# Spreading the norms' scales with two one-pass products, and loading the pooling weights in mid-kernel

## The chip, the core and the metric

The kernel runs on one core of one Trainium2 chip. The metric is the device time of one execution in microseconds, from the runs of the same kernel on that core; the median of three runs is quoted. Beside them stands one profiled execution, whose trace is read below. Its times are counted from the start of its span.

## The reference

One inference step of a two-layer trunk on 1024 prompt positions and 8 x 8 sample positions, width 1024, all in fp32. Cut to what matters here:

```python
def rms_norm(x, g):
    y = x * lax.rsqrt(jnp.mean(x * x, axis=-1, keepdims=True) + RMS_EPS)
    return y * g

# per layer l, x is (positions, 1024):
h = rms_norm(x, ng[MIX_PRE]);  y = mixer(h)          # even layer: pooling + convolution; odd: gated convolution
x = x + rms_norm(y, ng[MIX_POST])
h = rms_norm(x, ng[X_PRE]);    y = mem_attend(h)
x = x + rms_norm(y, ng[X_POST])
h = rms_norm(x, ng[FFN_PRE]);  y = conv_ffn(h)
x = x + rms_norm(y, ng[FFN_POST])

# the pooling head group of the even mixer ends in one 128 x 128 product per group g:
ya = einsum('bsgc,gcd->bsgd', pooled, w_pool) * pool_scale
```

So each position (a column in the kernel) has one scale per norm, and every norm multiplies 1024 channels by it.

## The kernel before, in words

Activations lie with the channels on the 128 partitions and the positions along the free axis. The positions are cut in two halves: half 0 has 512 prompt positions, half 1 has 512 prompt positions and the 64 samples (576, worked in two banks of 288). Three threads (`a` and `b` for the halves, `k` for the memory's keys and values) are Python generators. `schedule` (L461) runs them in an order written by hand (`SCRIPT`, L1457). Between pieces of matmul work, the norms, attention and convolutions run as background generators. When a background step is emitted depends on a planner, `Times` (L76): it keeps an estimated clock for each engine, and `after` (L319) lets a generator wait until TensorE's planned clock has come up to the planned end of a tile. `proj` (L499) calls the background after chunks 1, 3 and 5 of a product (`MID`, L1642). The planner prices a product at L171 by the type of its stationary operand, `max(n * 1.667 + 5, 222)` ns for fp32 and `max(n * 0.451 + 2.5, 107)` for fp32r. Those are constants of the program and decide order alone.

Weight products are done with fp32 numbers cut into two fp32r parts (a rounded high part, and the rest), in three one-pass products (`mm3`, L488). Each weight tile is loaded by SyncE into the ring `w` (10 buffers) as `wraw`, copied to `whi` by ScalarE, and subtracted to `wlo` by VectorE.

A norm goes through `rstd_gen` (L536). The sum of squares `acc` is summed over partitions by products with a column of ones (`psum_s`, L550), which puts the sums of 128 positions on 128 partitions and leaves 4 or 5 columns. `rsqrt` (L575) makes `r` out of them in eleven small VectorE instructions. The products at L557 then spread `r` back: the stationary operand is one column of `r` broadcast to 128 x 128, the moving one is the identity `ident`, and the result holds each position's scale on all partitions. It goes to the bank `psum_n`, or to `psum_r` and from there by ScalarE to the tile `rs`. These are native fp32 products, and each shows in the trace as two instructions. `prenorm_gen` (L608), `postnorm_gen` (L649), `ln_gen` (L871), `last_gen` (L1397) and `kv_thread` (L1001) use it, for 28 norms in all. The tiles of the norms are called `h` both where the scaled value is made and where it is cut in two.

The pooling weights (256 KB) are loaded into a constant tile `wp` by GpSimd's queue in `run` (L1435, L1436). In `even_in`, half 0 cuts them into `wpool` (L762, L763) with `split` (L529) after the background work has ended, and the four pooling products (L770) follow at once. The other temporary tiles come from `tt` (L360), a ring of 11 buffers.

In `run`, `cst` (all constants, the identity among them) is loaded by ScalarE's queue. VectorE then fills `ones` and `zero`, and ScalarE runs a first small activation on `zero` (L1430). Each engine takes its instructions in the order in which the program emits them.

Of the kernel before, what the change touches and what calls it, by code (L numbers as in the profile page):

```python
# [4 lines left out]
F32 = mybir.dt.float32  # L5
F32R = mybir.dt.float32r
I32 = mybir.dt.int32
AF = mybir.ActivationFunctionType
ALU = mybir.AluOpType
AX = mybir.AxisListType  # L10

P = 128
# [63 lines left out]
class Times:  # L76
# [58 lines left out]
    def run(self, engine, ns, outs, ins, port=False):  # L135
        t = self.start(engine, outs, ins)
        if engine == "sync":
            self.free["sync"] = t + 60
            self.free["dma"] = max(self.free["dma"], t) + ns
            t, engine = max(self.free["dma"], t + ns) + 2000, "dma"  # L140
        else:
            if port:
                t = self.port(engine, t, ns)
            t += ns
            self.free[engine] = t
        for a in ins:
            self.last[a.tensor.name] = max(self.last.get(a.tensor.name, 0.0), t)
        for a in outs:
            self.note(a, t, engine)
# [142 lines left out]
class Trunk:  # L292
# [243 lines left out]
    def rstd_gen(self, acc, n, out, dim, eps):  # L536


        nc = self.nc
        offs = []  # L540
        o = 0
        while o < n:
            offs.append((o, min(P, n - o)))
            o += P
        nt = len(offs)
        yield from self.after(acc)
        ps = self.bank(name="psum_s")
        for j, (o, m) in enumerate(offs):
            o = o + m - P
            nc.tensor.matmul(ps[:, j:j + 1], lhsT=acc[:, o:o + P], rhs=self.ones[:, 0:1])  # L550
        r = self.rsqrt(ps[:, :nt], nt, dim, eps)
        yield from self.after(r)
        for o, m in self.spans(n):
            pb = self.bank(name="psum_r") if out is not None else self.norm_bank()
            for i in range(o // P, -(-(o + m) // P)):
                w = min(P, o + m - i * P)
                nc.tensor.matmul(pb[:, i * P - o:i * P - o + w], lhsT=r[:, i:i + 1].to_broadcast([P, P]),  # L557
                                 rhs=self.ident[:, P - w:], start=True, stop=True)
            if out is not None:
                nc.scalar.activation(out=out[:, o:o + m], in_=pb[:, :m], func=AF.Copy)  # L560
        yield
        return (pb if out is None else out)[:, :n]
# [145 lines left out]
    def even_in(self, th, H, ops, cat):  # L708
        nc = self.nc
        us = [None] * 4  # L710
        cbs = [self.s([P, 2, H.n], F32, "cb") for _ in range(2)]
        ready = [0] * 4
        L = CW - 1
        th.bg.append(self.conv_gen(H, us, cbs, ready))
        self.rank[th.bg[-1]] = CONV_RANK + H.i
        th.bg.append(self.ln_gen(H, cbs, ready, cat))
        for c in (0, 3, 2, 1):
            yield ("slots", 1)
            w = self.take(("in_even", 4 + c))
            b1 = self.proj(w, ops, H)  # L720
            yield "pe"
            w = self.take(("in_even", 8 + c))
            b2 = self.proj(w, ops, H)
            sg = self.tt(name="sg")
            for b, (o, n) in zip(b2, H.banks):
                nc.scalar.activation(out=sg[:, o:o + n], in_=b[:, :n], func=AF.Sigmoid)
            u = self.s([P, L + NP + NB * (L + 8) if H.i else L + NP], F32, "u")
            us_ = None
            if H.i == 0:
                nc.gpsimd.memset(u[:, 0:L], 0.0)  # L730
            else:
                nc.gpsimd.tensor_copy(out=u[:, 0:L], in_=self.carry_u[:, c, :])
                us_ = u[:, L + NP:].rearrange("p (b t) -> p b t", t=L + 8)
                nc.sync.dma_start(us_[:, :, 0:L], self.t["st_conf"][:, c])
            for bi, bo, n, to, kind in H.pieces:
                dst, like = u[:, L + to:L + to + n], lambda a: a
                if kind == "s":
                    dst, like = us_[:, :, L:], lambda a: a.rearrange("p (b t) -> p b t", t=8)
                nc.vector.tensor_tensor(out=dst, in0=like(b1[bi][:, bo:bo + n]), in1=like(sg[:, to:to + n]),
                                        op=ALU.mult)  # L740
            b1 = b2 = None
            if H.i == 0:
                nc.gpsimd.tensor_copy(out=self.carry_u[:, c, :], in_=u[:, NP:NP + L])
            else:
                nc.gpsimd.dma_start(self.t["o_conf_p"][:, c], u[:, NP:NP + L])
                nc.gpsimd.dma_start(self.t["o_conf_s"][:, c], us_[:, :, 8:])
            us[c] = (u, u[:, :L + NP], us_)
            del u
            yield "phase"
        pls = []  # L750
        for g in range(4):
            yield ("slots", 1)
            w = self.take(("in_even", g))
            b1 = self.proj(w, ops, H)
            pls.append(self.s([P, 2, H.n], F32R, "pl"))
            self.pool_chunk(th, H, g, b1, pls)
            yield "pe"
        ops.clear()
        yield "phase"
        yield "bg"  # L760
        if H.i == 0:
            self.wpool = self.s([P, 2, 4, P], F32R, "wpool")  # L762
            self.split(self.wpool.t, self.wp)  # L763
        for g in range(4):
            yield ("slots", 1)
            sc = self.const("pool_scale", g)
            x, c = pls[g], cat[g]
            for o, n in H.banks:
                b = self.bank()
                self.mm3(b[:, :n], (self.wpool[:, 0, g, :], self.wpool[:, 1, g, :]),  # L770
                         (x[:, 0, o:o + n], x[:, 1, o:o + n]), True, True)
                nc.scalar.activation(out=c[:, 0, o:o + n], in_=b[:, :n], func=AF.Copy, scale=sc)
                nc.vector.scalar_tensor_tensor(out=c[:, 1, o:o + n], in0=b[:, :n], scalar=sc,
                                               in1=c[:, 0, o:o + n].bitcast(F32), op0=ALU.mult, op1=ALU.subtract)
            pls[g] = x = None
        if H.i:
            self.wpool = None
        yield "pe"
# [640 lines left out]
    def run(self):  # L1419
        nc, t = self.nc, self.t  # L1420
        C = self.C
        self.cst = C.tile([P, N_CONST], F32, name="cst")
        nc.scalar.dma_start(self.cst, t["consts"])
        self.ident = self.const("ident", 0, P)
        self.ones = C.tile([P, P], F32, name="ones")
        nc.vector.memset(self.ones, 1.0)
        self.zero = C.tile([P, 1], F32, name="zero")
        nc.vector.memset(self.zero, 0.0)
        first = C.tile([P, 1], F32, name="first")
        nc.scalar.activation(out=first, in_=self.zero, func=AF.Square)  # L1430
        self.carry_u = C.tile([P, 4, CW - 1], F32, name="carry_u")
        self.carry_a = C.tile([P, 4, PB], F32, name="carry_a")
        self.carry_g = C.tile([P, 8, 2], F32, name="carry_g")
        self.carry_f = C.tile([P, NF, 2], F32, name="carry_f")
        self.wp = C.tile([P, 4, P], F32, name="wp")  # L1435
        nc.gpsimd.dma_start(self.wp, t["wpool"])  # L1436
        a, b, k = Thread("a"), Thread("b"), Thread("k")
        self.threads = [k, a, b]
        a.gen = self.half_thread(a, self.halves[0])
        b.gen = self.half_thread(b, self.halves[1])  # L1440
        k.gen = self.kv_thread(k)
        by_name = {"a": a, "b": b, "k": k}
        todo = {n: phases(n) for n in by_name}
        script = []
        for word in SCRIPT.split():
            n, _, times = word.partition("*")
            for _ in range(int(times or 1)):
                self.order += todo[n].pop(0)
                script.append(by_name[n])
        assert not any(todo.values()), todo  # L1450
        self.schedule(script)
        while any(th.bg for th in self.threads):
            self.background()
            self.idle(100)
# [26 lines left out]
def phases(thread):  # L1481

    if thread == "k":
        return [[]] + [[("%s%d" % (n, l), c + i) for i in range(2)] for l in range(2) for n in "kv" for c in range(0, 8, 2)]
    return [[]] + layer_units(0) + layer_units(1)
# [326 lines left out]
```

## Time and profile before

| what | value |
|---|---|
| median of 3 runs | 3032.44 us (3029.54 to 3032.87) |
| the profiled execution's own time | 3032.25 us |
| its span | 3030.5 us |
| mean granted TensorE clock | 0.992 |
| TensorE busy | 2962.4 us (98%), 17866 instructions |
| VectorE busy | 1936.1 us (64%) |
| ScalarE busy | 1286.3 us (42%) |
| GpSimd busy | 103.2 us (3%) |

PE is TensorE's matmul, PEld its weight load, DVE VectorE, ACT ScalarE, POOL GpSimd, SP SyncE; SPq and ACTq are the queues that issue their transfers. Nearly every instruction is recorded by one helper (L202), so the tiles' names tell the groups apart. A product's instructions overlap their neighbours: a burst of x instructions costs the time from its start to the start of what follows it, which is less than x times its mean.

### The profile page before, as it was taken

What the parts mean: (1) busy time and instruction counts of PE and PEld (TensorE: products, weight loads), DVE (VectorE), ACT (ScalarE), POOL (GpSimd) and SP (SyncE); (2) the same over time, 40 slices, a digit from 0 to 9 for tenths busy, and PEclk for the clock granted to TensorE, in tenths of its full rate; (3) what the DMA queues carried; (4) which work ended last, traced back from release to release, by engine and by line L of the source; (5) the groups of instructions that cost most, each with busy time, mean ns of one, the idle gap of its engine ahead of it and who ended that gap; (6) DMA issues with size and microseconds to landing.
All of it is one profiled execution on the core that took longest, in us unless ns stands there. A gap on an engine that the chain in (4) does not pass through costs nothing. (4 is left out here: it accounts for less than half of the span.)

```text
span 3030.5 us, 44401 instructions
## 1 busy us (share of the span) xinstructions
PE 2962.4 (98%) x17866; PEld 2686.9 (89%) x17866; DVE 1936.1 (64%) x3275; ACT 1286.3 (42%) x2027; POOL 103.2 (3%) x404
## 2 busy tenths in 40 slices
PE   7999999999999999999999999999999999999997
PEld 5998789888888999999988899989888989999997
DVE  7999955747737545557748374567477475555558
ACT  5333374555543432333334333545555444333332
POOL 1110000000000000000000000000000000000000
PEclk9999999999999999999999999999999999999998
DMA  6657535524543222223333332243355233222233
GB/s 239 205 155 254 192 115 207 206 94 161 177 167 128 86 84 91 91 79 111 111 114 133 98 133 89 81 167 115 115 174 169 89 128 103 81 83 84 91 99 134
DMA packets 126493, 396.27 MB, mean 131 GB/s; under 512 B 21152, under 2 KB 31840, under 8 KB 126288
## 3 DMA queue, kind: packets, MB, share of 16 engines
q1 hardware_dynamic: 120144, 372.67, 36.8%
q0 software_dynamic: 6000, 20.45, 1.8%
q8 instruction: 140, 2.29, 0.3%
q14 instruction: 65, 0.53, 0.1%
q10 hardware_dynamic: 144, 0.33, 0.0%
HBM read 338.08 MB, written 55.31 MB: 130 GB/s over the span
## 5 line engine op out<-in xcount | busy, mean ns | idle before, releaser
L202 PE MATMUL b<-h,whi 128*128 128x288 f32 (+1 forms) x6720 | 1618.2, 332 | 22.3 <-DVE h L202 17.1
L202 PEld LDWEIGHTS b<-h,whi 128*128 128x128 f32 x6720 | 1142.0, 190 | 120.6 <-DVE h L202 21.4
L202 PE MATMUL b<-h,wlo 128*128 128x288 f32 (+1 forms) x3360 | 1110.5, 331 | 0.8 <-DVE wlo L202 0.8
L202 DVE TENSOR_TENSOR wlo<-wraw,whi 128x1024 fp32r<-128x1024 f32 x396 | 484.8, 1224 | 337.7 <-ACT whi L202 333.2
L202 PEld LDWEIGHTS b<-h,wlo 128*128 128x128 f32 x3360 | 637.7, 190 | 52.2 <-DVE wlo L202 1.5
L202 ACT ACTIVATE whi<-wraw 128x1024 fp32r<-128x1024 f32 x432 | 451.2, 1049 | 246.9 <-PE b L202 227.8
L202 PE MATMUL b<-z,whi 128*128 128x288 f32 (+1 forms) x2112 | 503.4, 329 | 1.3 <-ACT z L202 0.9
L202 PEld LDWEIGHTS b<-z,whi 128*128 128x128 f32 x2112 | 357.3, 188 | 32.9 <-ACT z L202 1.2
L202 PE MATMUL b<-z,wlo 128*128 128x288 f32 (+1 forms) x1056 | 347.5, 329 | 0.0
L202 DVE SCALAR_TENSOR_TENSOR cv<-ext,cst,cv 128x512 f32<-128x512 f32 (+1 forms) x208 | 166.7, 801 | 275.9 <-ACT cv L202 272.0
L202 DVE TENSOR_TENSOR y<-y,b 128x288 f32<-128x288 f32 (+1 forms) x480 | 243.1, 530 | 86.7 <-PE b L202 84.5
L202 PEld LDWEIGHTS b<-z,wlo 128*128 128x128 f32 x1056 | 198.6, 188 | 15.9
L202 DVE SCALAR_TENSOR_TENSOR cb<-u,cst,cb 128x512 f32<-128x512 f32 x360 | 187.3, 597 | 0.4
L202 PE MATMUL b<-o,whi 128*128 128x288 f32 (+1 forms) x768 | 185.1, 332 | 1.3 <-ACT o L202 0.9
L202 PE MATMUL b<-cat,whi 128*128 128x288 f32 (+1 forms) x768 | 183.7, 330 | 0.2 <-DVE cat L202 0.2
L202 ACT ACTIVATE ext<-b 128x224 f32<-128x224 f32 (+3 forms) x176 | 65.2, 397 | 262.8 <-PE b L202 262.8
L202 DVE TENSOR_TENSOR acc<-acc,sq 128x576 f32<-128x576 f32 (+3 forms) x188 | 129.2, 690 | 57.4 <-ACT sq L202 54.8
L202 ACT ACTIVATE y<-b 128x288 f32<-128x288 f32 (+1 forms) x144 | 67.0, 472 | 216.4 <-PE b L202 216.4
L202 PEld LDWEIGHTS b<-o,whi 128*128 128x128 f32 x768 | 131.1, 190 | 12.7 <-ACT o L202 1.1
L202 PEld LDWEIGHTS b<-cat,whi 128*128 128x128 f32 x768 | 130.5, 189 | 12.4 <-DVE cat L202 0.6
L202 ACT ACTIVATE z<-z 128x512 fp32r<-128x512 f32 (+1 forms) x88 | 58.0, 659 | 194.9 <-DVE z L202 194.9
L202 PE MATMUL b<-o,wlo 128*128 128x288 f32 (+1 forms) x384 | 127.1, 331 | 0.0
(162 smaller groups left out, 2655.3 us busy)
## 6 DMA issues: line engine op xcount, KB each, us to landing
wraw<-w SPq DMA_DIRECT2D x464, 512.0 KB, 3.5
cache<-cache_k SPq DMA_DIRECT2D x32, 512.0 KB, 4.4
cache<-cache_v SPq DMA_DIRECT2D x32, 512.0 KB, 4.5
xd<-x SPq DMA_DIRECT2D x20, 576.0 KB, 6.9
x<-xd SPq DMA_DIRECT2D x20, 576.0 KB, 6.6
xd<-x SPq DMA_DIRECT2D x20, 512.0 KB, 6.0
x<-xd SPq DMA_DIRECT2D x20, 512.0 KB, 6.9
lo_in_even<-wlo POOLq DMA_DIRECT2D x12, 512.0 KB, 5.8
```

The costliest lines, as they stand in the source:

```text
L202: r = f(*args, **kw)
```

## The change

`rstd_gen` now copies `r` to an fp32r tile `rh` and the rest, `r - rh`, to `rl` on VectorE, and waits for `rl`. Each spreading product becomes two one-pass fp32r products, of `rh` and of `rl`, added in the bank. The moving operand is `unit`, an fp32r copy of the identity made on VectorE in `run`, ahead of `ones` and `zero`. The constant tile `wp` and its load on GpSimd's queue go. `even_in` takes a tile of the ring instead and loads the pooling weights on SyncE's queue just ahead of the split that reads them.

```diff
         r = self.rsqrt(ps[:, :nt], nt, dim, eps)
-        yield from self.after(r)
+        rh, rl = (self.R.tile([P, 8], F32R, tag=t, name=t)[:, :nt] for t in ("rh", "rl"))
+        nc.vector.tensor_copy(out=rh, in_=r)
+        nc.vector.tensor_tensor(out=rl, in0=r, in1=rh.bitcast(F32), op=ALU.subtract)
+        yield from self.after(rl)
         for o, m in self.spans(n):
             pb = self.bank(name="psum_r") if out is not None else self.norm_bank()
             for i in range(o // P, -(-(o + m) // P)):
                 w = min(P, o + m - i * P)
-                nc.tensor.matmul(pb[:, i * P - o:i * P - o + w], lhsT=r[:, i:i + 1].to_broadcast([P, P]),
-                                 rhs=self.ident[:, P - w:], start=True, stop=True)
+                for q in (rh, rl):
+                    nc.tensor.matmul(pb[:, i * P - o:i * P - o + w], lhsT=q[:, i:i + 1].to_broadcast([P, P]),
+                                     rhs=self.unit[:, P - w:], start=q is rh, stop=q is rl)
...
         if H.i == 0:
+            wp = self.tt(name="wp")[:, :4 * P].rearrange("p (g d) -> p g d", g=4)
+            self.nc.sync.dma_start(wp, self.t["wpool"])
             self.wpool = self.s([P, 2, 4, P], F32R, "wpool")
-            self.split(self.wpool.t, self.wp)
+            self.split(self.wpool.t, wp)
...
         self.ident = self.const("ident", 0, P)
+        self.unit = C.tile([P, P], F32R, name="unit")
+        nc.vector.tensor_copy(out=self.unit, in_=self.ident)
         self.ones = C.tile([P, P], F32, name="ones")
...
-        self.wp = C.tile([P, 4, P], F32, name="wp")
-        nc.gpsimd.dma_start(self.wp, t["wpool"])
```

## Rows read from the trace of the kernel before

**Rows 1.** The page, part 1: busy us by engine (share of the span), instructions.
```profile
PE 2962.4 (98%) x17866; PEld 2686.9 (89%) x17866; DVE 1936.1 (64%) x3275; ACT 1286.3 (42%) x2027; POOL 103.2 (3%) x404
```

**Rows 2.** Waits of the whole span: us in total, times, longest us.
```profile
PE b L202 <- DVE h L202: 17.1, 11, 2.5
```

**Rows 3.** Window: length; busy us (instructions) PE, PEld, DVE, ACT, POOL; granted clock, DMA share, GB/s.
```profile
2040.00:2044.00 4.00, 4.00 (x22) 4.00 (x23) 3.72 (x15) 0.35 (x1) 0.00 (x0) 0.63 0.00 0
```

**Rows 4.** Groups by form: instructions, shapes, count | busy us, mean ns | idle before.
```profile
L202 PEld LDWEIGHTS b<-h,whi 128*128 128x128 f32 x6720 | 1142.0, 190 | 120.6 <-DVE h L202 21.4 <-ACT whi L202 4.1 <-ACT h L202 1.4
...
L202 PEld LDWEIGHTS psum_r<-cst,r 128*128 128x128 f32 x130 | 16.4, 190 | 1.7 <-DVE r L202 0.8
...
L202 PEld LDWEIGHTS psum_n<-cst,r 128*128 128x128 f32 x110 | 15.9, 218 | 4.6 <-DVE r L202 4.5
```

**Rows 5.** Timeline around one norm, 310 to 316: start us, us, engine, operation.
```profile
310.81 0.95 PE L202 MATMUL psum_s<-ones,acc 128*128 128x1 f32 x8
...
311.62 3.70 PE L202 MATMUL b<-mop,wraw 128*128 128x256 f32 x16
...
313.58 0.16 DVE L202 SCALAR_TENSOR_TENSOR r<-q,r 128x4 f32<-128x4 f32 x1
...
315.16 1.05 PE L202 MATMUL psum_n<-cst,r 128*128 128x128 f32 x8
...
316.05 7.07 PE L202 MATMUL b<-mop,wraw 128*128 128x256 f32 x32
```

**Rows 6.** Timeline of PE around twelve fp32r products of 256 columns, 2089.8 to 2091.4.
```profile
2089.86 1.60 PE L202 MATMUL b<-kv,qx 128*128 128x256 f32 x12
...
2091.29 0.40 PE L202 MATMUL b<-h,whi 128*128 128x512 f32 x1
```

**Rows 7.** Timeline of the start, 0 to 15.
```profile
0.74 0.40 ACTq L202 DMA_DIRECT2D cst<-consts  x1
...
1.18 1.28 ACT L202 ACT_TABLE_LOAD   x1 [1.18 <-PEq L1800]
...
6.00 0.63 ACT L202 ACTIVATE acc<-x 128x512 f32<-128x512 f32 x1 [3.32 <-DMA x<-x]
...
7.18 0.69 DVE L202 TENSOR_TENSOR acc<-acc,sq 128x512 f32<-128x512 f32 x1 [6.17 <-ACT sq L202]
...
8.61 4.67 DVE L202 TENSOR_TENSOR acc<-acc,sq 128x512 f32<-128x512 f32 x6 [0.73 <-ACT sq L202]
...
13.33 1.86 PE L202 MATMUL psum_s<-ones,acc 128*128 128x1 f32 x8 [13.33 <-DVE acc L202]
```

**Rows 8.** Transfers: issues, KB each, median us from issue to landing.
```profile
kvraw<-kd SPq DMA_DIRECT2D x16, 256.0 KB, 4.2
...
cst<-consts ACTq DMA_DIRECT2D x1, 320.0 KB, 5.4
...
wp<-wpool POOLq DMA_DIRECT2D x1, 256.0 KB, 7.1
```

**Rows 9.** Timelines of four engines around the pooling products, 249 to 265.
```profile
249.57 2.45 SPq L202 DMA_DIRECT2D wraw<-w  x2
...
264.67 23.82 SPq L202 DMA_DIRECT2D wraw<-w  x7
...
252.92 0.62 ACT L202 ACTIVATE wpool<-wp 128x512 fp32r<-128x512 f32 x1
...
255.91 0.70 DVE L202 TENSOR_TENSOR wpool<-wp,wpool 128x512 fp32r<-128x512 f32 x1
...
256.67 2.60 PE L202 MATMUL b<-pl,wpool 128*128 128x512 f32 x10 [1.10 <-DVE wpool L202]
```

**Rows 10.** Timeline of DVE in the tail.
```profile
3015.64 0.16 DVE L202 TENSOR_TENSOR q<-q,y 128x3 f32<-128x3 f32 x1
...
3015.83 0.16 DVE L202 SCALAR_TENSOR_TENSOR r<-q,r 128x3 f32<-128x3 f32 x1
...
3026.32 0.82 DVE L202 TENSOR_TENSOR x<-x,h 128x288 f32<-128x288 f32 x2
```

## Prediction

> **What bounds the kernel.** I read the page first: TensorE is busy for 2962.4 us of 3030.5 (98%), VectorE for 64% [rows 1]. So a part of the change is worth what it adds to or takes from TensorE's queue, or from the few places where that queue stands still. I looked for these next, in the waits: inside the kernel TensorE waits longest for a norm's `h`, 17.1 us in 11 waits [rows 2]. Such a wait costs more than its length: after the longest (2.5 us, just before 2040) the granted clock was 0.63 over the next 4 us, so most of that stretch ran at the lower of its two levels, 1.2 GHz [rows 3]. Besides these there are the start, 13.33 us before the first product [rows 7], and the tail, where VectorE ends the run. Then I went to the groups of the tiles `psum_r` and `psum_n` and to the timeline around one norm, for the price of a spreading product.
>
> **The spreading products.** Before, these are 130 instructions for `psum_r` and 110 for `psum_n`, counted by their weight loads [rows 4], 240 in all, so 120 native products of two instructions. After, there are two one-pass products for each: 240 again. No instruction goes; the question is only what one costs. Before: eight run from 315.16 to 316.05, so 0.89 / 8 = 0.111 us each [rows 5]. What limits them? The sums of `psum_s` move one column instead of 128 and still cost (311.62 - 310.81) / 8 = 0.101 us each [rows 5]. Loading 128 columns of weights is nearly the whole price, and moving the columns adds 0.01. The change keeps one load for each instruction, and a recorded load has 190 ns for fp32r (`b<-h,whi`) as for native fp32 (`psum_r`) [rows 4]; the 218 of `psum_n` holds the slow loads of the start and the tail. I therefore take 0.101 for the new instruction, a saving of 0.010 x 240 = **-2.4 us**, nearly all on TensorE's path.
>
> No row shows an fp32r product of under 256 columns. At 256 it costs (2091.29 - 2089.86) / 12 = 0.119 us [rows 6], and 128 columns without a bound by loading would be half of that, 0.060: the lower end is 240 x (0.111 - 0.060) = -12.2 us. The upper end is that a one-pass product this narrow is run at the price of a whole native product, 0.222: +0.111 x 240 = +26.6 us. Both ends are rivals below. I stay near 0.101 because the one-column row and the equal loads both say that the load is the limit.
>
> A page of the Trainium skill counts otherwise. FP8 and Floating Point Precision, TensorE Precision Notes, states that true fp32 takes four passes through the array. At the 53.3 ns for 128 columns that the skill's page TensorE: Matmul & The Clock Gate gives (Wait — 56ns, not 53.3ns?), four passes are 213 ns, which agrees with 0.222 a product here, and by passes alone two one-pass products would save half: an estimate of 120 x 0.107 = 12.8 us. The one-column row speaks against counting passes: there the columns are gone and the price stays.
>
> **Two more VectorE instructions in each norm.** Small dependent instructions follow each other at 3015.83 - 3015.64 = 0.19 us [rows 10], so `rh` and `rl` put 0.4 us between `r` and the products. VectorE itself has room for 28 x 0.4 = 11 us at 64% busy [rows 1]. What counts is lateness, and behind these two on VectorE's queue stand the weights' `wlo` and the scaled `h`, 0.4 us later each time.
>
> In mid-kernel the products wait in TensorE's queue anyway. In the norm shown `r` is there at 313.74, and TensorE comes to its products at 315.16 [rows 5], a margin of 1.4 us. So 0.4 us is covered there as long as the products keep their place in the order. The planner's clock for the norm moves by about as much, and where that misses a place, the next one comes a few products later. I put the 11 waits for `h` [rows 2] on about six chains of two norms each; if every one of these norms came 0.4 later the cost would be 6 x 2 x 0.4 = 4.8 us. A changed order can also take waits away, and I bound that at -3, under a fifth of 17.1. With margins like the one shown I take **+1.5 us**, a third of the upper end.
>
> **Start.** Nothing covers the first norm: +0.4. The copy to `unit` waits for `cst`, which is issued at 0.74 and lands 5.4 us later [rows 7, 8], at about 6.15. `ones` and `zero` stand behind it on VectorE, and ScalarE's first activation behind `zero`, so ScalarE gets to the squares at about 6.9 rather than 6.00 [rows 7]. VectorE's first addition, at 7.18 before, then begins at about 8.1 and ends by 8.75. The other six began at 8.61 [rows 7], when the next squares were there: 0.15 us late. If ScalarE's table load (1.28) waits for `zero` too, the first addition comes at 9.4, and seven at 4.67 / 6 = 0.78 end at 14.9 instead of 13.3: +1.6. The other way, 256 KB fewer are under way in the first microseconds, and the six additions had waited 0.73 for their squares [rows 7], which bounds that gain. I take **+0.5** for the start (0.4 + 0.15, rounded), from 0.4 - 0.7 = -0.3 to 0.4 + 1.6 = +2.0. GpSimd's queue loses one issue and waits for nothing with it.
>
> **Pooling weights.** The new load is issued by SyncE behind the weight loads that end at 249.57 + 2.45 = 252.02 [rows 9]. It cannot stand behind the later ones, whose buffers come free only through work after the pooling. Landing: 4.2 us is the row of reads of the same 256 KB in mid-kernel, 7.1 that of this very load at the crowded start [rows 8]; I take 4.2, so 256.2. ScalarE's part (0.62) ends at about 256.85, VectorE's (0.70) at 257.55, against 255.91 + 0.70 = 256.61 before [rows 9]: **+0.9 us** on TensorE, which already waits here (1.10). The lower end is nothing: however early it lands, VectorE comes to its part only at 255.91. With 7.1 it is +3.9, and the gap is then long enough for the clock to fall as in [rows 3], 4 x 0.37 = 1.5 more: +5.4. Behind the split, ScalarE's queue holds the copies of the pooling results, which wait for TensorE anyway. SyncE's next weight loads came at 264.67 [rows 9], so none is late.
>
> **Tail.** The last norm's `r` is done at 3015.99, and from there VectorE runs nearly without a gap to 3027.1 [rows 10]. Two more instructions: **+0.4 us**.
>
> **Sum.** -2.4 + 1.5 + 0.5 + 0.9 + 0.4 = +0.9 us. The profiled execution's 3032.25 (span 3030.5 and 1.75 around it) becomes 3033.15; the median lies 0.2 higher, so I say **3033.3**. A measurement of this kernel tells a change from none at about 0.2%, 6 us. The forecast is no change that can be told. Its own range, with the bounds taken mostly together, is 3028 to 3040.
>
> **Rivals.**
> 1. *The one-pass product is not bound by its load* and costs 0.060: -12.2 in place of -2.4, 3033.3 - 9.8 = 3023.5, faster. For it: nothing narrower than 256 columns is on record. Against: the loads of 190 ns in either type, and the one-column sums. The skill has a rule on its side: TensorE: Matmul & The Clock Gate, Weight-path perf modes, says that fast weight loading is on for 128 weights of any input type but FP32; if fp32r counts as another type, loads shrink. The same table expects no gain from it for fp32, and the equal 190 ns agree with that. Chance 0.12.
> 2. *Narrow fp32r products run at the native price*, 0.222 each: +26.6 in place of -2.4 gives 3062.3, slower. Its place is every norm's burst: eight instructions in 1.8 us instead of 0.89. From 0.111 + (6 - 3.3) / 240 = 0.122 us an instruction on, it decides for slower, the other parts being +3.3. For it: every fp32r product of this kernel has 256 columns or more, so no row excludes it. Against: at 256 columns one costs only 0.119, and half the columns have no evident reason to cost more. Chance 0.11.
> 3. *The pooling weights come late* and the order slips against the norms' chains: landing in 7.1 us with the clock's fall gives +5.4 in place of +0.9, 3037.8, still inside 0.2%; with the chains' full 4.8 it is 3041.1, slower. Chance 0.10, half of it over the bound.
>
> **Numbers.** The forecast has 0.67. Faster: 0.12 from the first rival and 0.03 from the forecast's own low end (order) = 0.15. Slower: 0.11 from the second, 0.05 from the third, 0.05 from the forecast's high end = 0.21. Within 0.2%: 0.64. The range takes in the first rival and the third and leaves out the second: 3022 to 3042.
>
> **What would show it.** In the changed profile: 240 instructions on `psum_n` and `psum_r` with bursts of eight at 0.8 to 0.9 us (0.5 is the first rival, 1.8 the second); two VectorE instructions behind each `r`; ScalarE's squares at about 6.9 and the first spreading product about 0.5 later; the pooling split on ScalarE at about 256.2 instead of 252.92; TensorE's waits for `h` still near 17 us. A sum of these waits that moves by more than 5 us either way would make the forecast wrong through order alone.

## The result: 0.56% slower, outside the range

The changed kernel took 3049.01 us in the median of four runs (3047.00 to 3051.74); the kernel before, beside it, 3031.95 (3029.54 to 3032.87). The ratio is 1.0056, with a 95% interval from 1.0044 to 1.0069: about 17 us slower. I had said 3033.3, with 3042 as the upper end.

The changed kernel's profiled execution took 3051.74 us, with a span of 3049.9, 19.4 more than before. The page, part 1:

```profile
PE 2972.6 (97%) x17866; PEld 2693.5 (88%) x17866; DVE 1945.5 (64%) x3332; ACT 1287.1 (42%) x2027; POOL 104.0 (3%) x403
```

TensorE has the same 17866 instructions and is busy for 10.2 us more [rows 1]; it stands still for 3049.9 - 2972.6 = 77.3 us against 68.1, which is 9.2 more. The two make up the 19.4. Longer at an equal count points to the clock: the mean granted clock fell from 0.992 to 0.987. VectorE got 57 instructions, 9.4 us of work, with 36% of its time free.

What TensorE waited for in the whole span (us in total, times, longest):

```profile
PE b L202 <- DVE h L202: 20.8, 16, 3.3
PE psum_s L202 <- DVE acc L202: 17.8, 5, 13.2
...
PE b L202 <- ACT pr L202: 2.1, 1, 2.1
PE b L202 <- ACT wpool L202: 1.6, 1, 1.6
PE b L202 <- DVE cat L202: 1.5, 1, 1.5
PE b L202 <- ACT q L202: 1.5, 1, 1.5
```

The waits for `h` rose from 17.1 to 20.8 [rows 2], in 16 places rather than 11. Waits for `pr`, `q` and ScalarE's part of `wpool` appear that before had not, and that for `cat` grew from 0.2. One group is gone; in the kernel before it was:

```profile
PE b L202 <- ACT qx L202: 3.0, 3, 1.7
```

Behind several of the waits the clock falls. Three stretches of the kernel before (first fence) and the stretches of the changed kernel in which it is at the same stages (second); after the busy times stands the granted clock:

```profile
600.00:620.00 20.00, 17.61 (x102) 14.95 (x101) 11.69 (x20) 12.82 (x21) 0.28 (x2) 1.00 0.22 79
...
2525.00:2540.00 15.00, 13.01 (x85) 12.55 (x84) 8.70 (x11) 4.66 (x8) 0.61 (x4) 0.89 0.22 72
255.00:275.00 20.00, 18.90 (x82) 14.94 (x81) 17.10 (x32) 10.40 (x16) 1.19 (x3) 1.00 0.48 181
```

```profile
610.00:630.00 20.00, 16.67 (x83) 14.10 (x83) 10.77 (x21) 11.37 (x22) 0.28 (x2) 0.91 0.20 66
...
2540.00:2555.00 15.00, 11.60 (x57) 10.21 (x57) 10.43 (x14) 3.75 (x7) 0.00 (x0) 0.77 0.21 71
255.00:275.00 20.00, 17.62 (x63) 13.48 (x62) 15.88 (x29) 8.86 (x14) 1.60 (x3) 0.83 0.54 176
```

Each of the three lost both ways, in TensorE's busy time and in its clock, and got less done in the same time. The first of them close up, before and after, with the wait for `h` in it and the window right behind that wait:

```profile
603.80 0.50 PE L202 MATMUL b<-h,whi 128*128 128x512 f32 x1 [1.61 <-DVE h L202]
...
603.80:612.00 8.20, 8.20 (x43) 6.95 (x44) 4.98 (x7) 5.29 (x7) 0.28 (x2) 1.00 0.03 9
```

```profile
616.11 0.50 PE L202 MATMUL b<-h,whi 128*128 128x512 f32 x1 [3.33 <-DVE h L202]
...
616.10:620.00 3.90, 3.89 (x18) 3.76 (x19) 1.50 (x2) 2.69 (x3) 0.28 (x2) 0.57 0.00 0
```

The wait grew from 1.61 to 3.33 us. Behind the shorter one the granted clock was 1.00 up to 612, behind the longer one it was 0.57 up to 620. So the loss is spread over a dozen places, and the questions are what these have in common, and whether the new instructions or the new order make it.

**The products.** A burst of eight before (first fence) and in the changed kernel (second), timeline of PE, first row of the burst and first row behind it:

```profile
2045.46 1.05 PE L202 MATMUL psum_n<-cst,r 128*128 128x128 f32 x8
2046.27 0.51 PE L202 MATMUL b<-h,whi 128*128 128x288 f32 x2
```

```profile
2061.99 0.22 PE L202 MATMUL psum_n<-unit,rh 128*128 128x128 f32 x1
...
2062.83 0.35 PE L202 MATMUL b<-h,whi 128*128 128x288 f32 x1
```

0.81 us before, 0.84 after: 0.101 and 0.105 an instruction. A burst of ten takes 1.03 in both kernels. The weight loads are alike too: 130 for `psum_r`, 110 for `psum_n`, median 192 ns (190 before). The burst that the prediction priced, among products `b<-mop,wraw`, took 0.89 [rows 5] and takes 1.03 now (first row, and the first row behind it):

```profile
320.03 0.41 PE L202 MATMUL psum_n<-unit,rh 128*128 128x128 f32 x1
...
321.06 0.86 PE L202 MATMUL b<-mop,wraw 128*128 128x256 f32 x3
```

Leaving out the first of the 28 bursts, the last two and the one near 550, the other 24 take 22.3 us together before and 22.8 in the changed kernel.

**The start** (timeline):

```profile
6.02 0.23 DVE L202 CAST unit<-cst 128x128 fp32r<-128x128 f32 x1 [6.02 <-DMA cst<-consts]
...
6.54 0.61 ACT L202 ACTIVATE acc<-x 128x512 f32<-128x512 f32 x1
...
7.70 5.47 DVE L202 TENSOR_TENSOR acc<-acc,sq 128x512 f32<-128x512 f32 x7 [1.31 <-ACT sq L202]
...
13.23 1.87 PE L202 MATMUL psum_s<-ones,acc 128*128 128x1 f32 x8 [13.23 <-DVE acc L202]
```

ScalarE comes to the squares 0.54 later than before [rows 7], but now the seven additions run in one piece. The first product comes at 13.23 instead of 13.33, and VectorE begins the first scaled `h` at 19.35 in both kernels: the start cost nothing.

**The pooling weights** (timelines of SP, ACT, DVE and PE):

```profile
250.74 0.43 SPq L202 DMA_DIRECT2D wp<-wpool  x1
...
256.78 0.63 ACT L202 ACTIVATE wpool<-wp 128x512 fp32r<-128x512 f32 x1 [3.04 <-DMA wp<-wpool]
...
258.21 0.68 DVE L202 TENSOR_TENSOR wpool<-wp,wpool 128x512 fp32r<-128x512 f32 x1
...
257.47 0.73 PE L202 MATMUL b<-pl,wpool 128*128 128x512 f32 x2 [1.64 <-ACT wpool L202]
258.95 3.36 PE L202 MATMUL b<-pl,wpool 128*128 128x512 f32 x7 [0.75 <-DVE wpool L202]
```

The load was issued 1.3 us earlier than I assumed and took 6.0 rather than 4.2. By this stage the changed kernel is 5 us behind. That looks like the price of the late load, and I took it for that at first.

### The profile page after: what moved, and what is told of

The parts are those of the page before. It is cut to its first block, busy times and chain, and to the rows that moved or that the text cites. A ratio compares the mean times of both kernels' runs of the same rounds, so it can differ in the third digit from the quotient of the medians.

```text
span 3049.9 us, 44454 instructions
## 1 busy us (share of the span) xinstructions
PE 2972.6 (97%) x17866; PEld 2693.5 (88%) x17866; DVE 1945.5 (64%) x3332; ACT 1287.1 (42%) x2027; POOL 104.0 (3%) x403
## 5 line engine op out<-in xcount | busy, mean ns | idle before, releaser
L202 PE MATMUL b<-h,whi 128*128 128x288 f32 (+1 forms) x6720 | 1620.7, 332 | 25.8 <-DVE h L202 20.8
L202 PEld LDWEIGHTS b<-z,wlo 128*128 128x128 f32 x1056 | 198.5, 188 | 15.9
```

The lines of the kernel that those rows point to most:

```text
L202: r = f(*args, **kw)
```

## The experiments

Two theories to begin with. *Order*: the program that lays out the work (the planner, `Times`) is told the new norm's costs and lays out another order, and this costs the time. *Instructions*: `r`'s 0.4 us cost it, whatever the order.

**The change taken apart.** Four kernels. The first is the change with the load back at the start (32 bytes of room come from writing ScalarE's first activation into a state tile); the second has the load's move alone:

```
e1:  changed kernel, but
+        self.wp = C.tile([P, 4, P], F32, name="wp")
+        nc.gpsimd.dma_start(self.wp, t["wpool"])
...
e2:  kernel before, but
+            wp = self.tt(name="wp")[:, :4 * P].rearrange(...)
+            self.nc.sync.dma_start(wp, self.t["wpool"])
...
```

> The changed norms with the pooling weights loaded at the start as before (the order of the engines stays the changed kernel's). Late load costs what the two traces say (about 4.3 us, with the clock's fall behind it): 4 to 5 us faster than the changed kernel, so about 12 us, 0.4%, slower than the kernel before. If the load cost only the 0.9 us of the forecast, about 16 us slower than before.

Measured: 3050.24 us, ratio 1.0061 (1.0048 to 1.0073). No faster than the changed kernel.

> The kernel before with the load of the pooling weights alone moved into mid-kernel; norms and TensorE's order as before. Late load costs 4.3 us with the clock's fall: ratio 1.0014, TensorE at half clock between 257 and 265 us. If it costs 0.9 us: ratio 1.0003. In neither theory more than 6 us.

Measured: 3033.26 us, ratio 1.0005 (0.9996 to 1.0014): about 2 us. My reading of the pooling stage fell with these two. In the third kernel, which has native products and the early load, the same stage shows (DVE, then PE):

```profile
258.08 0.68 DVE L202 TENSOR_TENSOR wpool<-wp,wpool 128x512 fp32r<-128x512 f32 x1
...
258.82 3.42 PE L202 MATMUL b<-pl,wpool 128*128 128x512 f32 x8 [3.01 <-DVE wpool L202]
```

There the weights have long been there, but VectorE's part of the split stands 2.2 us later on its queue than before [rows 9], behind four more steps of `cb` (a running sum of the convolution). The order alone makes this wait.

The third kernel computes with the instructions of the kernel before, and only tells the layout program the new costs; the fourth is its reverse, with the change's instructions (emitted past the layout program, `.eng`) and the native costs told:

```
e4:
+        for port in (False, True):
+            self.times.run("vector", 68 + nt * 1.045, [r], [r], port)
...
-                nc.tensor.matmul(pb[...], lhsT=r[...], rhs=self.ident[...])
+                nc.tensor.eng.matmul(ap, lhsT=rb, rhs=self.ident[...])
+                for _ in range(2):
+                    self.times.run("tensor", max(w * 0.451 + 2.5, 107), [ap], [rb])
...
e5:
+        nc.vector.eng.tensor_copy(out=rh, in_=r)
+        nc.vector.eng.tensor_tensor(out=rl, in0=r, in1=rh.bitcast(F32), op=ALU.subtract)
...
+                self.times.run("tensor", max(w * 1.667 + 5, 222), ...)
...
```

> The instructions of the kernel before, native products and early load, in the order that the planner lays out when it is told the changed norm's costs (two VectorE steps of about 0.18 us and two products of 0.107 us in place of 0.222). Theory order: the lost 12 us are there without one new instruction, ratio 1.004 (1.003 to 1.005), with lost clock near 35 us-equivalents in place of 26. Theory instructions (0.4 us later in every norm, whatever the order): ratio 1.000.

Measured: 3047.49 us, ratio 1.0054 (1.0040 to 1.0067). 16.5 us without one new instruction.

> The changed norm's instructions (two VectorE steps, two one-pass products), pooling weights early, in the order of the kernel before: the planner is told the native norm's costs. Theory order: no change that can be told, ratio 1.000 (0.999 to 1.001). Theory instructions: the 12 us are here, ratio 1.004; waits of TensorE for `h` longer by some 5 us than the 17.1 of before.

Measured: 3035.41 us, ratio 1.0015 (1.0007 to 1.0024): 4.4 us. TensorE's waits for `h` are 15.9 there, so not longer; of the 2.7 us that its profiled span is longer, 2.6 are busy time.

The order is the large part, then. The sum holds too:

> All of the change's instructions, its late load too, in the order of the kernel before. If the three runs add up, the norm's instructions (4.4 us) and the late load (2.3 us) give 3037.7 us, ratio 1.002, and the other 11 us of the changed kernel are order. Theory instructions: as the changed kernel, 1.0056.

Measured: 3038.49 us, ratio 1.0025 (1.0015 to 1.0035). 4.4 + 2.3 = 6.7 was expected, 7.2 came. The recorded orders bear the design out: on TensorE and VectorE the run with the order alone (e4) has the changed kernel's sequence, one for one but for the new instructions, and the two with the order kept (e5, e3) have that of before.

The parts don't add up to the 17.1 us of the change, though. In the new order, the norm's instructions and the late load add only 17.1 - 16.5 = 0.6; taking the new order out of the whole change gives back 17.1 - 7.2 = 9.9. So the order's price is 10 to 16.5 us, by the end from which one takes it.

**What in the told costs turns the order.** The kernel before again, with other costs told:

```
s_steps:
+        for port in (False, True):
+            self.times.run("vector", 68 + nt * 1.045, [r], [r], port)
s_late_x, s_early_x (x in ns, early with a minus):
+        self.times.note(r, self.times.written[r.tensor.name][-1][2] + x, "vector")
```

> The instructions of the kernel before; the planner is told of the two VectorE steps alone (0.36 us later, and VectorE busy for 0.14 us more), not of the cheaper products. If the steps turn the order: ratio 1.005 as in the run with the order alone. If the told price of the products does it: 1.000.

Measured: 3047.08 us, ratio 1.0052 (1.0039 to 1.0066). The two VectorE steps, told alone, are enough; the products' told price isn't needed.

> The instructions of the kernel before; the planner is told that each norm's `r` is there 0.362 us later, without any VectorE time. If lateness alone spoils the order: 1.005. If the order is a matter of where the small shifts fall: anything between 0.997 and 1.005, no relation to the size of the shift.

Measured: 3054.39 us, ratio 1.0075 (1.0063 to 1.0088): more than either expectation.

> The same with 0.724 us. If the loss grows with the told lateness: ratio over 1.005, up to 1.010. If it is a matter of where shifts fall: between 0.997 and 1.005, in no order with the run of 0.362.

Measured: 3056.57 us, ratio 1.0084 (1.0070 to 1.0098): hardly more than for half the lateness.

> The instructions of the kernel before; the planner is told that each norm's `r` comes 0.110 us later. Up to 0.100 us its order of TensorE is that of before; here one norm of the second half (near 2040 us) slips behind two more background products and what follows is laid out anew. Theory order: one slip costs one lengthened wait and a fall of the clock, 2 to 6 us, ratio 1.0005 to 1.002, all behind 2000 us. If one slip re-lays enough to cost the whole: 1.005.

Measured: 3040.01 us, ratio 1.0026 (1.0015 to 1.0038), 9 us and thus more than one wait's price. The windows 2375 to 2395 of this kernel and of the kernel before:

```profile
2375.00:2395.00 20.00, 15.23 (x82) 13.86 (x82) 11.45 (x15) 9.86 (x18) 0.10 (x1) 0.74 0.15 53
```

```profile
2375.00:2395.00 20.00, 20.00 (x137) 19.04 (x136) 8.08 (x11) 8.90 (x14) 0.28 (x2) 1.00 0.26 85
```

Here a chain of the samples' attention, over `cache`, `so` and `o`, lost its cover: five waits of 4.77 us together, and the clock fell to 0.74 over the 20 us, where before TensorE had run through.

> The same with 0.6 us earlier: three norms move ahead by two background products, the rest stands. If the norm's place alone makes the waits, this takes some away: ratio 0.998 to 1.000. If the order of before is no better than its neighbours by more than chance: 0.998 to 1.003.

Measured: 3034.54 us, ratio 1.0010 (1.0000 to 1.0019): no gain.

> The same with 1.0 us earlier: the whole order is laid out anew. If told lateness is what costs, an early norm gains or costs nothing: 0.997 to 1.001. If any new layout costs, because the planner's other settings were fitted to the one of before: 1.003 to 1.008, as for the late ones.

Measured: 3056.42 us, ratio 1.0083 (1.0069 to 1.0097). Here TensorE comes to the norms' products before `r` is there; these waits are 15 us together, against 4.3 before (first fence):

```profile
PE psum_n L202 <- DVE r L202: 4.3, 2, 2.2
```

```profile
PE psum_r L202 <- DVE r L202: 7.5, 12, 0.8
PE psum_n L202 <- DVE r L202: 7.4, 9, 2.2
```

So the loss doesn't grow with the told lateness. Every one of these orders that differed much from that of before lost 9 to 25 us, in either direction: 589 to 2726 of TensorE's 17866 places hold another product (by tile and shape) in them, and 50 in the run with 0.6 us early.

**What in the order costs.** In the kernel before, six norms' products start 0.07 to 0.14 us behind `r` on TensorE; in the changed kernel and in most of the orders that lost, they stand one place (0.8 or 1.4 us) further back. So I suspected their place, and put it back with one line:

```
-        yield from self.after(rl)
+        yield from self.after(r)
```

> The whole change with one line altered: the norm's thread comes back for its products when `r` is there, not when `rl` is; the planner is told all else as it is. If what costs is that the products go to the next place behind the background products, 0.7 to 1.4 us later, they keep their places, TensorE stands some 0.2 us in front of several of them, and the time is that of the run with all instructions in the old order: ratio 1.0025, 10 us faster than the changed kernel. If the place of the products is not the cause: 1.005 to 1.006.

Measured: 3049.12 us, ratio 1.0056 (1.0042 to 1.0069), although the products are back directly behind `r`. So that place alone is not what the changed kernel pays for. What is left is told best by comparing this kernel with e3, which has the same instructions and, but for a stretch near 600 us, the same order on TensorE, and is 10.6 us faster. VectorE in e5, whose order here is that of e3 and of before (first fence), and in the kernel with the one line altered (second), in the same stage:

```profile
2510.24 0.81 DVE L202 SCALAR_TENSOR_TENSOR h<-x,cst,rs 128x576 f32<-128x576 f32 x1
2511.43 1.54 DVE L202 SCALAR_TENSOR_TENSOR cv<-ext,cst,cv 128x512 f32<-128x512 f32 x2 [0.39 <-ACT cv L202]
...
2529.83 2.76 DVE L202 TENSOR_TENSOR h<-h 128x576 fp32r<-128x576 f32 x4
2532.51 1.22 DVE L202 TENSOR_TENSOR wlo<-wraw,whi 128x1024 fp32r<-128x1024 f32 x1
```

```profile
2522.16 1.54 DVE L202 SCALAR_TENSOR_TENSOR cv<-ext,cst,cv 128x512 f32<-128x512 f32 x2 [1.12 <-ACT cv L202]
...
2540.55 1.42 DVE L202 TENSOR_TENSOR h<-h 128x576 fp32r<-128x576 f32 x2
2541.89 0.81 DVE L202 SCALAR_TENSOR_TENSOR h<-x,cst,rs 128x576 f32<-128x576 f32 x1
2542.62 0.75 DVE L202 TENSOR_TENSOR h<-h 128x576 fp32r<-128x576 f32 x1
2543.29 1.22 DVE L202 TENSOR_TENSOR wlo<-wraw,whi 128x1024 fp32r<-128x1024 f32 x1
2544.43 0.75 DVE L202 TENSOR_TENSOR h<-h 128x576 fp32r<-128x576 f32 x1
```

Read the second against the first. In e5 one scaling of `h` (0.81) stands ahead of `cv` and leaves a gap of 0.39. In the other kernel the layout program thought VectorE 0.36 us later, put that scaling behind `cv` (another running sum of a convolution), and the gap in which it would have fitted stands empty: 1.12. From there on the scalings are one behind. The one that is left over comes 20 us later, when TensorE is at these very products: four parts of `h` in one piece (2.76 us) become four with a scaling and a weights' split between. TensorE waits for them three times, where e5 has one wait (e5's row first, then the other kernel's):

```profile
2530.64 0.40 PE L202 MATMUL b<-h,whi 128*128 128x288 f32 x1 [1.87 <-DVE h L202]
```

```profile
2541.36 0.40 PE L202 MATMUL b<-h,whi 128*128 128x288 f32 x1 [1.87 <-DVE h L202]
...
2543.43 0.40 PE L202 MATMUL b<-h,whi 128*128 128x288 f32 x1 [0.74 <-DVE h L202]
...
2545.23 0.61 PE L202 MATMUL b<-h,whi 128*128 128x288 f32 x1 [1.14 <-DVE h L202]
```

Two runs tested this theory from both ends, VectorE's clock in the layout program alone:

```
v_clock_told:    kernel before, but
+        self.times.free["vector"] += 364
v_steps_untold:  changed kernel, but
+        nc.vector.eng.tensor_copy(out=rh, in_=r)
+        nc.vector.eng.tensor_tensor(out=rl, ...)
+        yield from self.after(r)
...
```

The second also lets the norm's thread come back at `r`, as the run before it does; against that run (3049.12), what is new is that the two VectorE steps, and with them the later `rl`, are not told.

> The instructions of the kernel before; after each norm's `r` the planner's clock of VectorE alone is put on by 0.364 us, `r` itself stays in time, so that the norm's products keep their places on TensorE. If it is VectorE's order that costs (a scaling of `h` that no longer fits its gap and lands later between the parts that TensorE waits for): slower by what the last run lost against the one in the old order, 9 to 11 us, ratio 1.003 to 1.0035, with the waits near 1018 and 2541 of that run. If VectorE's order is not the cause: 1.000.

Measured: 3045.70 us, ratio 1.0051 (1.0037 to 1.0064): 14 us, more than expected, from VectorE's told clock alone. TensorE's order is that of before except between 568 and 630 us. Its page, part 1, and TensorE's waits for `h`:

```profile
PE 2969.4 (98%) x17866; PEld 2690.7 (88%) x17866; DVE 1936.1 (64%) x3275; ACT 1287.3 (42%) x2027; POOL 101.2 (3%) x404
```

```profile
PE b L202 <- DVE h L202: 22.0, 15, 3.3
```

Its span is 3044.5, so TensorE stands for 75.1 us, 7.0 more than before, and is busy for 7.0 more with the same instructions: half of the loss are the waits, half is the clock behind them (mean granted clock 0.989 for 0.992). Of the waits' 7.0 us, 2.4 are the pooling weights (3.48 for 1.10), 1.8 the place near 1018, 1.2 that near 2541, and 1.3 that near 609.

> The whole change; the planner is told all of it but the two VectorE steps (the products' new cost and the late load are told). If VectorE's told time is the cause: as the run with all instructions in the old order, ratio 1.0025, 10 us faster than the changed kernel. If the products' told cost or the load's place in the layout plays a part: over 1.004.

Measured: 3037.50 us, ratio 1.0023 (1.0012 to 1.0033). Not telling the layout program of two instructions gives back 11 of the 17 us, and TensorE's recorded order is that of before throughout.

VectorE's told clock is thus enough to make the loss, but it is not the only way to it. The runs with `r` told 0.362 and 0.724 us late leave that clock alone and lose 23 and 25 us. Their recorded order differs from that of before on VectorE as well as on TensorE, so they don't say which of the two costs.

No version beats the kernel before. Left open besides: whether other settings of the layout program would find an order as good as the old one for the new costs; none was tried.

## Why the prediction was wrong

- **Spreading products, -2.4.** About +0.5, by the 24 bursts. The mechanism fits, the price stays near that of the one-column sums and neither of the first two rivals came. The term was mis-sized because 0.111 is the price of the burst in [rows 5]; 16 of the 28 bursts before run at 0.101 to 0.103, so there was nothing to save in them, and the burst of [rows 5] itself became dearer. The Trainium skill, FP8 and Floating Point Precision, TensorE Precision Notes, counts four passes for true fp32; two one-pass products would have saved an estimated 12.8 us by that. The bursts of 0.81 and 0.84 decide against counting passes for loads this narrow.
- **Two more VectorE instructions, mid-kernel, +1.5: the step that failed.** I bounded what lateness and a changed order could cost at 4.8, by "six chains of two norms each" times 0.4 us, and put the slip on the norm's products on TensorE. The run with the order alone has 16.5. Three things were wrong in it. The slip, in the stage shown, is not the lateness told but the size of the work that misses its gap (0.8 us, or 1.2 with a weights' split). It happens on VectorE, whose 36% of free time I took for room, and it hits what is queued there for other purposes: the parts of `h` and the pooling weights' split, as the run with VectorE's clock told shows. And the waits bring about as much again in clock, which I had priced for the pooling stage alone. The changed kernel's waits for `pr`, `q` and `cat`, 5.1 us between 424 and 432, are not in that run; TensorE's own order differs there, and no run takes these apart. The instructions themselves, in the old order, cost about 4.4 with the tail's 0.4: a range up to 4.8 fitted these.
- **My watch was on the wrong row.** I had said that a sum of the waits for `h` moving by over 5 us would mean order. It moved by 3.7, and order it was, in the main: other waits had spread to `pr`, `q`, `cat` and `wpool`, and the clock hid the rest in the busy time. TensorE's idle time and its busy time at an equal instruction count would have shown it.
- **The margin of 1.4 us** in the norm shown was no pattern: six norms have 0.07 to 0.14. It didn't matter to the changed kernel, either: with the products put back to these places the changed kernel takes the same time, 3049.12 and 3049.01.
- **Start, +0.5.** ScalarE's squares came at 6.54, not 6.9, as `cst` landed at 6.02 and the copy took 0.23; the additions lost their gap, as the other bound had it. Nothing in all.
- **Pooling weights, +0.9.** Alone 2.3 (1.0005, 0.9996 to 1.0014, so not clear of none): inside my bounds of 0 to 5.4. In the changed order they are hidden (the early load, e1, was no faster), since VectorE's part of the split is late by itself. The third rival had this stage and the order together, but put the order's price at 4.8 again.
- **Tail, +0.4.** As said: the last two waits are 3.08 and 2.45 against 2.85 and 2.25.

## What to carry to other kernels

Where a program lays out the order from told costs, a cost term has two prices: what the instruction takes, and what the new order takes. Measure them apart: the old instructions with the new costs told, and the new instructions with the old. Here the second price was 16.5 us with the old instructions, or 10 taken out of the whole change, and the first 4.4 in the old order. In an order as tight as this one, look at the engine with free time first: a small step that misses its gap there comes back later, between the parts that the full engine waits for.

## What the runs showed of the hardware

In most bursts, an fp32r product of 128 columns costs what one instruction of a native fp32 product costs, 0.105 us against 0.101, so two for one is an even exchange; among the products `b<-mop,wraw` a burst of eight takes 1.03 us where the native one took 0.89. And added waits on TensorE cost about as much again in clock, taken together: in the run with VectorE's clock told, 7.0 us of waits came with 7.0 us of longer products, the granted clock in 600 to 620 being 0.91 where it had been 1.00 before. A single wait has no fixed price: behind the one of 1.61 us in the kernel before the clock stayed at 1.00, and behind that of 3.33 in the changed kernel it was 0.57.
